# A hybrid decoder trunk on one core: the tables of its S5 groups built for two batches at once, their third one copied, one scaling moved to ScalarE

## The chip, the cores and the metric

The kernel runs on one core of a Trainium2 chip. The metric is the device time of one execution in microseconds (us), lower is better. A core has a tensor engine (PE), a vector engine (DVE), a scalar engine (ACT), GpSimd (POOL) and a sync engine (SP), which here issues nearly all DMAs. Each engine works through its own instructions in order and waits for others by semaphores.

## What is computed

A trunk of two layers over 1040 tokens (16 learned ones ahead of 1024) of width 1024, in float32. Layer 0 mixes the tokens by RG-LRU heads (512 channels) and by 32 S5 groups of 16 channels with 64 complex states each; layer 1 by a Mamba-2 mixer. A squared-ReLU MLP follows each mixer. What the change touches is the S5 part and one line of the RG-LRU:

```python
# S5, group g: a complex diagonal recurrence over the tokens
mag = exp(a_re * dt);  ar, ai = mag * cos(a_im * dt), mag * sin(a_im * dt)
fr = ((ar - 1) * a_re + ai * a_im) / den;  fi = (ai * a_re - (ar - 1) * a_im) / den
bbar = (fr + i fi) * b            # input vectors, 64 states x 16 channels
s[t] = (ar + i ai) * s[t - 1] + bbar @ u[t]
y[t] = Re(c @ s[t]) + d * u[t]
# RG-LRU
a = exp(log_a);  mult = sqrt(-expm1(2 * log_a));  h[t] = a[t] * h[t - 1] + mult[t] * (i[t] * x[t])
```

## The kernel before, in words

Tokens lie in three ranges of 400, 384 and 256 columns. Every dense product is made of three float32r products of 12-bit halves (`mm3`, lines 162 to 164) with features on the partitions; weights are loaded by SP into three buffers (`wraw`), split on ACT (line 156) and on DVE or POOL (line 157).

The first mixer (`mixer0`) runs 36 units of the input projection (12 output tiles by three token ranges). The first four tiles are the S5 channels (u0 to u3), then come those of the RG-LRU (x0 to x3) and its gates (g0 to g3). Between the units the program emits the work of the 32 S5 groups in eight batches of four: `s5_tables` makes the matrices of a batch, `s5_batch` its states and outputs, `s5_tile` the gelu and gate of 128 channels (two batches), and `lru_tile` the recurrence of 128 LRU channels. When all is there, the mixers' output is split and the output projection (`ev_out`) follows.

An S5 batch takes eight tokens at a time (130 chunks). Its state is turned by a phasor so that a real scan does the recurrence: `Z` holds cos and sin of 131 rotations for the four groups, built by doubling (2, 4, 8, 16, 32, 64, then 3 more columns; lines 557 to 559; steps below 32 on DVE, the wider ones on POOL). The partitions are 64 real and 64 imaginary rows, and both halves hold the same rotations. Lines 574 to 582 scale the batch's input and output vectors (64 elements per partition, nine DVE instructions). Three tables of 512 elements follow (lines 590 to 592, three instructions each): E (input), F and G (output; G on DVE for the first two batches, on POOL for the six others). PE turns E into M2 (lines 603, 604) and the taps into M1 (line 618). In `s5_batch`, PE makes two products (lines 643, 644), DVE multiplies them with `Z` (lines 647 to 649), scans (651), POOL and DVE multiply by sin and cos again (653, 654), and PE sums M1, F and G products (661 to 663). The chunks travel through DRAM (`ud`, `yd`).

The order on each engine is set by a list scheduler at build time, from the emission order with a few shifts; SP's queue is in order too, so a DMA that waits holds up those behind it.

Of the kernel before, what the change touches and what calls it, by code (L numbers as in the profile page):

```python
# [78 lines left out]
class Trunk:  # L79
    def __init__(self, ctx, tc, A, out, dbg=None):  # L80
# [189 lines left out]
    def apply(self, wname, i, off, w, rb):  # L270
        """hi, lo <- split of rmsnorm(h) * w"""
# [10 lines left out]
    def split(self, wname, i, k, off, w):  # L282
        """hi, lo <- split of h[:, k] * w; the norm's factor per token is left to the products"""
# [20 lines left out]
    def final(self, i):  # L304
        """the last norm, to the output"""
# [19 lines left out]
    def follow(self, nxt, tls, i):  # L325
        """queues the norm that comes after the residual stream of token range i is complete"""
# [13 lines left out]
    def up_unit(self, tls, ws, i, f, pool, tag, rbs):  # L340
        """one tile of the hidden layer for one token range, in two parts"""
# [21 lines left out]
    def mlp(self, layer, tls, mp, ahead, nxt, ep=None, early=None, rbs=None):  # L363
        """ahead: weights of the first two tiles; nxt: weight of the norm that follows;
        ep, early, rbs: a pool for the first range's hidden tiles, those that are there, norm factors"""
# [23 lines left out]
        def do_down(parts, i, last=False):  # L389
            """parts: (weights, hidden) of one or two blocks"""  # L390
# [3 lines left out]
            for n in range(KT):  # L394
# [35 lines left out]
    def s5_params(self, pool, keep):  # L430
        """what does not depend on the data (in two steps)"""
# [37 lines left out]
        # powers of lambda: index d holds lambda^(8-d)  # L469
# [7 lines left out]
        def cmul(dst, a, b, n):  # L477
            """powers dst.. = powers a.. * power b"""
# [12 lines left out]
        # input factors  # L491
# [17 lines left out]
        # sign: -1 on the real rows, +1 on the imaginary rows  # L509
# [4 lines left out]
        # unit phasors over 8 * 2^n chunks, n = 0..7: rows cos, -sin, sin; modulus over 8 steps  # L514
# [20 lines left out]
    def s5_tables(self, pool, b):  # L535
        """matrices and rotations of the groups NG*b .. NG*b+NG-1 (in three steps)"""
        nc, s5 = self.nc, self.s5
        v, e = nc.vector, nc.gpsimd
        gs = slice(NG * b, NG * b + NG)
        S4 = [P, NG, 8, 16]  # L540
        S3 = [P, NG, 16]
        # rotations exp(i theta8 m), m = 0..130: rows cos, sin
        Z = pool.tile([P, 2, NG, 131], F32, name="s5Z", bufs=2)
# [24 lines left out]
        xa, xb, ya, yb = (bc[:, i] for i in range(4))
        bw = lambda q: q[:, gs].unsqueeze(2).broadcast_to(S3)
        sg, ng = s5["sg"][:, 0:1], s5["sg"][:, 1:2]  # L570
        x1 = pool.tile(S3, F32, name="s5x1")
        x2 = pool.tile(S3, F32, name="s5x2")
        x3 = pool.tile(S3, F32, name="s5x3")
# [920 lines left out]
```

## Time and profile before

| what | us |
|---|---|
| median of 3 runs (lowest, highest) | 2868.11 (2867.05, 2870.88) |
| span of the profiled execution, first to last instruction | 2866.7 |
| own time of the profiled execution | not listed apart from the three runs; from 0.4 to 4.2 above its span by these |
| PE busy | 2751.3 (96%) |
| DVE busy | 1884.3 (66%) |
| ACT busy | 917.6 (32%) |
| POOL busy | 720.4 (25%) |

The page cuts the span into 40 slices of 71.7 us and gives the busy share of each in tenths. `PEclk` is the clock granted to the tensor engine in tenths of full speed. Spans of matmuls overlap in PE's pipeline, and those of short DVE instructions overlap a little too, so sums of single spans are above the busy time of a stretch.

### The profile page before, as it was taken

Reading aid. Unit: us, or ns where it says so; the run is one execution under the profiler, and the core shown is the slowest. Engines: PE = TensorE matmul, PEld = TensorE weight load, DVE = VectorE, ACT = ScalarE, POOL = GpSimd, SP = SyncE. Lnnn points to the kernel's source line nnn. Section 1 sums busy time; section 2 is a strip of 40 time slices with the busy share of each in tenths; the row PEclk is TensorE's granted clock in tenths of the full one; section 3 lists DMA queues with packets and bytes.
Section 4 is the critical chain, followed back from the end, with each engine's and each line's share of the span. In section 5 each row is a group of like instructions: output and inputs, shape, how many; then the busy total and the mean of one; then the engine's idle time right before and its main releaser. Section 6 shows DMA issues by size and latency. Waiting matters only on the chain.

```text
span 2866.7 us, 45283 instructions
## 1 busy us (share of the span) xinstructions
PE 2751.3 (96%) x17625; PEld 2684.1 (94%) x17625; DVE 1884.3 (66%) x4127; ACT 917.6 (32%) x1926; POOL 720.4 (25%) x879
## 2 busy tenths in 40 slices
PE   7877999999999999999999999999989999999998
PEld 7866999999999999899999999998889999999998
DVE  9999655555555555977867768677894555555554
ACT  4354542111211112454434434335452111121113
POOL 4555111101101011242333323334441011110112
PEclk9888999999999999999999999999999999999999
DMA  4111311110101111031212212213311111011111
GB/s 145 60 43 44 117 48 52 49 60 30 60 30 60 48 42 43 20 102 48 77 51 68 72 58 73 63 47 105 109 50 61 41 49 59 30 60 35 55 48 59
DMA packets 118919, 170.00 MB, mean 59 GB/s; under 512 B 17072, under 2 KB 51632, under 8 KB 118704
## 3 DMA queue, kind: packets, MB, share of 16 engines
q1 hardware_dynamic: 118416, 166.95, 18.1%
q8 instruction: 138, 2.26, 0.3%
q14 instruction: 77, 0.63, 0.1%
q10 hardware_dynamic: 288, 0.15, 0.0%
HBM read 158.34 MB, written 8.72 MB: 58 GB/s over the span
## 4 chain that ended last, share of the span: by engine, by line
PE 76%; DVE 17%; ACT 2%; issue 2%; DMA 2%; POOL 1%; SPq 0%; DVEq 0%; ACTq 0%; POOLq 0%
PE mm L163 23%; PE mm L162 23%; PE mm L164 23%; DVE xbc L1071 2%; DMA csb<-csd 1%; PE mm L1181 1%; PE sm L1185 1%; PE mm L1178 1%; DVE lo L288 1%; PE sm L1144 1%; PE sm L250 1%; PE sm L233 1%; DVE s5tt L591 1%; DVE wlo L157 0%; DVE h L697 0%
## 5 line engine op out<-in xcount | busy, mean ns | idle before, releaser
L162 PE MATMUL mm<-hi,whi 128*128 128x256 f32 (+2 forms) x2400 | 788.6, 329 | 9.2 <-ACT whi L156 8.5
L164 PE MATMUL mm<-hi,wlo 128*128 128x256 f32 (+2 forms) x2400 | 772.9, 322 | 3.2 <-POOL wlo L157 3.2
L163 PE MATMUL mm<-lo,whi 128*128 128x256 f32 (+2 forms) x2400 | 774.3, 323 | 1.2 <-POOL lo L280 0.6
L400 DVE TENSOR_TENSOR h<-h,mm 128x384 f32<-128x384 f32 (+1 forms) x720 | 369.0, 513 | 301.5 <-PE mm L164 299.5
L162 PEld LDWEIGHTS mm<-hi,whi 128*128 128x128 f32 x2400 | 457.5, 191 | 14.6 <-ACT whi L156 8.9
L164 PEld LDWEIGHTS mm<-hi,wlo 128*128 128x128 f32 x2400 | 456.8, 190 | 4.2 <-POOL wlo L157 3.9
L357 POOL TENSOR_TENSOR s<-s 128x384 f32<-128x384 f32 (+2 forms) x192 | 161.8, 843 | 1188.7 <-DVE s L356 946.3
L163 PEld LDWEIGHTS mm<-lo,whi 128*128 128x128 f32 x2400 | 456.1, 190 | 3.9 <-POOL lo L280 0.9
L163 PE MATMUL mm<-hl,dhi 128*128 128x384 f32 (+2 forms) x1440 | 459.5, 319 | 0.0
L164 PE MATMUL mm<-hh,dlo 128*128 128x384 f32 (+2 forms) x1440 | 459.4, 319 | 0.0
L162 PE MATMUL mm<-hh,dhi 128*128 128x384 f32 (+2 forms) x1440 | 459.3, 319 | 0.1
L156 ACT CAST dhi<-wraw 128x512 fp32r<-128x512 f32 x120 | 68.9, 620 | 653.7 <-PE mm L163 574.8
L162 PEld LDWEIGHTS mm<-hh,dhi 128*128 128x128 f32 x1440 | 271.9, 189 | 0.3 <-DVE h L400 0.3
L164 PEld LDWEIGHTS mm<-hh,dlo 128*128 128x128 f32 x1440 | 272.0, 189 | 0.0
L163 PEld LDWEIGHTS mm<-hl,dhi 128*128 128x128 f32 x1440 | 271.9, 189 | 0.0
L163 PE MATMUL mm<-lo,uhi 128*128 128x384 f32 (+2 forms) x768 | 245.3, 319 | 0.0
L164 PE MATMUL mm<-hi,ulo 128*128 128x384 f32 (+2 forms) x768 | 245.0, 319 | 0.0
L162 PE MATMUL mm<-hi,uhi 128*128 128x384 f32 (+2 forms) x768 | 244.9, 319 | 0.0
L1071 DVE SCALAR_TENSOR_TENSOR xbc<-s,cols,xbc 128x400 f32<-128x400 f32 (+2 forms) x288 | 202.5, 703 | 24.4 <-ACT xbc L1069 22.2
L358 ACT CAST hh<-s 128x384 fp32r<-128x384 f32 (+2 forms) x192 | 92.3, 480 | 384.4 <-POOL s L357 384.0
L359 DVE TENSOR_TENSOR hl<-s,hh 128x384 fp32r<-128x384 f32 (+2 forms) x192 | 99.5, 518 | 145.5 <-ACT hh L358 143.5
L356 DVE SCALAR_TENSOR_TENSOR s<-mm,rb 128x384 f32<-128x384 f32 (+2 forms) x192 | 98.9, 515 | 142.7 <-PE mm L164 139.5
(374 smaller groups left out, 4566.6 us busy)
## 6 DMA issues: line engine op xcount, KB each, us to landing
wraw<-in_mlp_up SPq DMA_DIRECT2D x128, 256.0 KB
wraw<-in_mlp_down SPq DMA_DIRECT2D x128, 256.0 KB
wraw<-in_ssd_in SPq DMA_DIRECT2D x120, 256.0 KB
csb<-csd SPq DMA_DIRECT2D x64, 256.0 KB
sa<-ecd SPq DMA_DIRECT2D x128, 64.0 KB
wraw<-in_ssd_out SPq DMA_DIRECT2D x32, 256.0 KB
wraw<-in_ev_in SPq DMA_DIRECT2D x24, 256.0 KB
wraw<-in_ev_out SPq DMA_DIRECT2D x18, 256.0 KB
```

Source lines behind the costliest of these rows:

```text
L156: nc.scalar.copy(hi[:, s], raw)
L162: nc.tensor.matmul(pt, lhsT=whi, rhs=xhi, start=first, stop=False)
L163: nc.tensor.matmul(pt, lhsT=whi, rhs=xlo, start=False, stop=False)
L164: nc.tensor.matmul(pt, lhsT=wlo, rhs=xhi, start=False, stop=last)
L233: nc.tensor.matmul(st[:l, 508 + i:509 + i], lhsT=a[:, o:o + l], rhs=self.ones, start=j == 0, stop=j == len(accs) - 1)
L250: self.nc.tensor.matmul(st[:, o:o + l], lhsT=y[:l, i:i + 1].broadcast_to([l, P]), rhs=self.ident[:l, :l], start=True, stop=True)
L356: nc.vector.scalar_tensor_tensor(out=r, in0=pt[:, :w], scalar=0.0, in1=rbs[i], op0=ALU.max, op1=ALU.mult)
L357: nc.gpsimd.tensor_tensor(out=sq, in0=r, in1=r, op=ALU.mult)
L358: nc.scalar.copy(hh, sq)
L359: nc.vector.tensor_tensor(out=hl, in0=sq, in1=hh.bitcast(F32), op=ALU.subtract)
L400: nc.vector.tensor_tensor(out=hs, in0=hs, in1=pt[:, :w], op=ALU.add)
L1071: v.scalar_tensor_tensor(out=ot, in0=raw[:, k:k + w], scalar=cw(k), in1=ot, op0=ALU.mult, op1=ALU.add)
```

## The change

- The vectors (old lines 574 to 582) are scaled once for all 32 groups, by `s5_vectors`: three ACT and six DVE instructions of 512 elements. One DMA of 1 MB brings them, in place of eight.
- The rotations of two batches are built at once (`s5_rotations`, called for even batches): the first batch on partitions 0 to 63, the second on 64 to 127, all steps on DVE. ACT makes a third row, minus sin, and four DMAs per pair copy the halves into the two batches' `Z`; the sign that line 648 applied is in that row now, so that line becomes a plain product.
- G is F with its partition halves exchanged: two DMAs per batch copy it.
- In `lru_tile` the scaling by 0.5 plus 0.5 (line 720) moves from DVE to ACT.
- The descriptor scratch of the program is set to 1024 bytes; comments are dropped, which moves line numbers.

```diff
+    def s5_vectors(self, pool):
...
+        nc.scalar.activation(out=xb, in_=xb, func=AF.Copy, scale=sg)
+        nc.scalar.activation(out=ya, in_=ya, func=AF.Copy, scale=ng)
+        nc.scalar.activation(out=yb, in_=yb, func=AF.Copy, scale=-1.0)
+        v.tensor_tensor(out=ta, in0=xa, in1=bw(s5["fi"]), op=ALU.mult)
+        v.tensor_tensor(out=tb, in0=xb, in1=bw(s5["fi"]), op=ALU.mult)
+        v.tensor_tensor(out=xa, in0=xa, in1=bw(s5["fr"]), op=ALU.mult)
+        v.tensor_tensor(out=xa, in0=xa, in1=tb, op=ALU.add)
+        v.tensor_tensor(out=xb, in0=xb, in1=bw(s5["fr"]), op=ALU.mult)
+        v.tensor_tensor(out=xb, in0=xb, in1=ta, op=ALU.subtract)
+
+    def s5_rotations(self, pool, b):
...
+        ph = pool.tile([P, 8, 3, NG], F32, name="s5phh")
+        for r in range(2):
+            g = NG * (b + r)
+            nc.scalar.copy(ph[r * H:(r + 1) * H], s5["ph"][r * H:(r + 1) * H, :, :, g:g + NG])
+        Z = pool.tile([P, 3, NG, 131], F32, name="s5Zh")
...
         while m < 131:
             l = min(m, 131 - m)
             S = [P, 2, NG, l]
...
-            e = v if m < 32 else nc.gpsimd
-            e.tensor_tensor(out=t1[:, :, :, :l], in0=Z[:, ::-1, :, 0:l], in1=pn, op=ALU.mult)
-            e.tensor_tensor(out=dst, in0=src, in1=pc, op=ALU.mult)
-            e.tensor_tensor(out=dst, in0=dst, in1=t1[:, :, :, :l], op=ALU.add)
+            v.tensor_tensor(out=t1[:, :, :, :l], in0=Z[:, 1::-1, :, 0:l], in1=pn, op=ALU.mult)
+            v.tensor_tensor(out=dst, in0=Z[:, 0:2, :, 0:l], in1=pc, op=ALU.mult)
+            v.tensor_tensor(out=dst, in0=dst, in1=t1[:, :, :, :l], op=ALU.add)
...
+        nc.scalar.activation(out=Z[:, 2], in_=Z[:, 1], func=AF.Copy, scale=-1.0)
+        for r in range(2):
+            q = self.rot[b + r] = pool.tile([P, 2, NG, 131], F32, name="s5Z", bufs=2)
+            nc.sync.dma_start(q[:H], Z[r * H:(r + 1) * H, 0:2])
+            nc.sync.dma_start(q[H:], Z[r * H:(r + 1) * H, 0:3:2])
...
-        v.tensor_scalar(out=xb, in0=xb, scalar1=sg, scalar2=None, op0=ALU.mult)
-        v.tensor_tensor(out=x1, in0=xa, in1=bw(s5["fr"]), op=ALU.mult)
-        v.tensor_tensor(out=x3, in0=xb, in1=bw(s5["fi"]), op=ALU.mult)
-        v.tensor_tensor(out=x1, in0=x1, in1=x3, op=ALU.add)
-        v.tensor_tensor(out=x2, in0=xb, in1=bw(s5["fr"]), op=ALU.mult)
-        v.tensor_tensor(out=x3, in0=xa, in1=bw(s5["fi"]), op=ALU.mult)
-        v.tensor_tensor(out=x2, in0=x2, in1=x3, op=ALU.subtract)
-        v.tensor_scalar(out=ya, in0=ya, scalar1=ng, scalar2=None, op0=ALU.mult)
-        v.tensor_scalar(out=yb, in0=yb, scalar1=-1.0, scalar2=None, op0=ALU.mult)
...
-        G = table("s5G", dn, yb, ya, ALU.subtract, v if b < 2 else e, "s5tt", 2)
+        G = pool.tile(S4, F32, name="s5G", bufs=2)
+        nc.sync.dma_start(G[:64], F[64:])
+        nc.sync.dma_start(G[64:], F[:64])
...
-            v.scalar_tensor_tensor(out=w2[sl], in0=v3(vb), scalar=ng, in1=Sn[sl], op0=ALU.mult, op1=ALU.mult)
+            v.tensor_tensor(out=w2[sl], in0=v3(vb), in1=Sn[sl], op=ALU.mult)
...
-            v.tensor_scalar(out=q[i], in0=q[i], scalar1=0.5, scalar2=0.5, op0=ALU.mult, op1=ALU.add)
+            nc.scalar.activation(out=q[i], in_=q[i], func=AF.Copy, scale=0.5, bias=0.5)
```

The scheduler makes a new order for the first mixer; behind it the engines' orders are as before. On DVE, at the tables of the third batch, there stood the last narrow doubling step and the vectors (`s5Z` is the batch's rotations, `s5bc` its vectors, `s5x` their products):

```order
L557 TENSOR_TENSOR s5t_1179<-s5Z,s5ph 128x8x16
L558 TENSOR_TENSOR s5Z<-s5Z,s5ph 128x8x16
L559 TENSOR_TENSOR s5Z<-s5Z,s5t_1179 128x8x16
L574 TENSOR_SCALAR s5bc<-s5bc,s5sg 128x64
L575 TENSOR_TENSOR s5x_1208<-s5bc,s5t_437 128x64
```

Now the wide steps of the second pair stand there, among the tables (`s5Zh` is the pair's rotations, `s5F`, `s5E` and `s5tt` the tables):

```order
L581 TENSOR_TENSOR s5t_1147<-s5Zh,s5phh 128x512
L582 TENSOR_TENSOR s5Zh<-s5Zh,s5phh 128x8x64
L610 TENSOR_TENSOR s5F<-s5t_409,s5bc 128x512
L583 TENSOR_TENSOR s5Zh<-s5Zh,s5t_1147 128x8x64
L612 TENSOR_TENSOR s5F<-s5F,s5tt 128x512
L581 TENSOR_TENSOR s5t_1147<-s5Zh,s5phh 128x8x3
```

The vectors have moved ahead, to one place before the first batch, and the wide steps have come over from POOL.

In SP's queue, between the second batch's chunks and the outputs of the first, there stood:

```order
L155 DMA wraw<-in_ev_in 128x512 x2
L768 DMA ud_112<-ux 128x1040
L666 DMA yd_113<-s5yg 8x16x130 x4
L565 DMA s5bc<-in_s5bc 128x4x64
L567 DMA s5dm<-in_s5dm 128x64
L632 DMA s5ug<-ud_110 128x1x130 x4
L155 DMA wraw<-in_ev_in 128x512 x3
```

Now the next weights stand among copies of G and `Z`, of which the second pair of `Z` copies (lines 589 and 590 after G) needs the buffer of the batch before:

```order
L654 DMA s5ug<-ud_110 128x1x130 x4
L634 DMA s5G<-s5F 64x512
L589 DMA s5Z<-s5Zh 64x1048
L590 DMA s5Z<-s5Zh 64x2x524
L635 DMA s5G<-s5F 64x512
L155 DMA wraw<-in_ev_in 128x512 x2
L589 DMA s5Z<-s5Zh 64x1048
L590 DMA s5Z<-s5Zh 64x2x524
L155 DMA wraw<-in_ev_in 128x512
```

Weight loads and chunk transfers that had DMAs from DRAM ahead of them now have copies ahead that wait for DVE and ACT.

## Rows read from the trace of the kernel before

**Rows 1.** The page, part 2: busy tenths in 40 slices of 71.7 us.

```profile
PE   7877999999999999999999999999989999999998
...
DVE  9999655555555555977867768677894555555554
...
PEclk9888999999999999999999999999999999999999
```

**Rows 2.** Windows: stretch, length, busy us (instructions) of PE, PEld, DVE, ACT, POOL, clock, DMA.

```profile
45.00:285.00 240.00, 189.65 (x1101) 174.90 (x1101) 224.53 (x503) 99.75 (x185) 130.34 (x141) 0.86 0.19 57
285.00:316.00 31.00, 29.82 (x176) 28.09 (x174) 24.41 (x47) 17.97 (x35) 5.29 (x5) 0.87 0.11 32
316.00:440.00 124.00, 120.30 (x759) 118.57 (x759) 71.20 (x145) 53.15 (x111) 21.38 (x20) 1.00 0.31 101
```

**Rows 3.** What PE waited for, 45 to 316 us: total us, times, longest.

```profile
PE mm L644 <- DVE ux L774: 10.1, 3, 6.3
PE sm L618 <- DVE s5kk L610: 7.7, 5, 2.2
...
PE sm L233 <- DVE sa L267: 0.2, 1, 0.2
```

**Rows 4.** Lines by form, DVE, 0 to 440 us: busy us, mean ns | idle before.

```profile
L580 DVE TENSOR_TENSOR s5x<-s5x,s5x 128x64 f32<-128x64 f32 x8 | 5.5, 684 | 0.0
...
L575 DVE TENSOR_TENSOR s5x<-s5bc,s5t 128x64 f32<-128x64 f32 x8 | 1.8, 224 | 0.0
```

**Rows 5.** Timeline, DVE at 160.5 us: start, span.

```profile
160.56 0.22 DVE L558 TENSOR_TENSOR s5Z<-s5Z,s5ph 128x64 f32<-128x64 f32 x1
160.69 0.22 DVE L577 TENSOR_TENSOR s5x<-s5x,s5x 128x64 f32<-128x64 f32 x1
```

**Rows 6.** Lines by form, DVE, 0 to 440 us: the narrow doubling steps.

```profile
L557 DVE TENSOR_TENSOR s5t<-s5Z,s5ph 128x16 f32<-128x16 f32 x8 | 4.4, 555 | 0.0
...
L558 DVE TENSOR_TENSOR s5Z<-s5Z,s5ph 128x16 f32<-128x16 f32 x8 | 1.4, 171 | 0.0
```

**Rows 7.** The same, the tables, the scaling and the line behind it.

```profile
L590 DVE TENSOR_TENSOR s5F<-s5t,s5bc 128x512 f32<-128x512 f32 x8 | 10.8, 1349 | 0.0
...
L592 DVE TENSOR_TENSOR s5F<-s5F,s5tt 128x512 f32<-128x512 f32 x8 | 6.2, 774 | 0.1
...
L721 DVE SCALAR_TENSOR_TENSOR l_tr<-h 128x400 f32<-128x400 f32 x4 | 4.9, 1224 | 0.1
...
L720 DVE TENSOR_SCALAR h<-h 128x400 f32<-128x400 f32 x4 | 3.1, 768 | 0.0
...
L721 DVE SCALAR_TENSOR_TENSOR l_tr<-h 128x384 f32<-128x384 f32 x4 | 2.2, 548 | 0.0
...
L720 DVE TENSOR_SCALAR h<-h 128x256 f32<-128x256 f32 x4 | 1.1, 285 | 0.0
```

**Rows 8.** Line 592's own instructions: duration min/median/max in ns, first and last start.

```profile
L592 DVE TENSOR_TENSOR s5F<-s5F,s5tt x8: 671/686/1411, 68.2 to 279.8; 128x512 f32<-128x512 f32 x8
L592 DVE TENSOR_TENSOR s5G<-s5G,s5tt x2: 681/686/692, 69.7 to 92.2; 128x512 f32<-128x512 f32 x2
```

**Rows 9.** Lines by form, POOL, 0 to 440 us: wide doubling steps, table G.

```profile
L559 POOL TENSOR_TENSOR s5Z<-s5Z,s5t 128x512 f32<-128x512 f32 x8 | 11.7, 1457 | 0.4
...
L590 POOL TENSOR_TENSOR s5G<-s5t,s5bc 128x512 f32<-128x512 f32 x6 | 8.7, 1450 | 0.6 <-issue 0.4
...
L591 POOL TENSOR_TENSOR s5tt<-s5t,s5bc 128x512 f32<-128x512 f32 x6 | 7.8, 1306 | 10.5 <-DVE s5F L592 10.5
...
L558 POOL TENSOR_TENSOR s5Z<-s5Z,s5ph 128x24 f32<-128x24 f32 x8 | 2.9, 362 | 19.1 <-DVE s5Z L559 7.7 <-DMA s5dm<-in_s5dm 4.7 <-DVE s5y L219 4.1
```

**Rows 10.** SP's queue: one issue with its time; its longest wait.

```profile
69.74 0.60 SPq L565 DMA_DIRECT2D s5bc<-in_s5bc  x1
SPq L155 <- DVE wlo L157: 122.4, 23, 26.2
```

**Rows 11.** The chain of waits: a transfer of 520 KB on the path.

```profile
316.06 3.38 DMA s5y<-yd
```

**Rows 12.** All waits, 0 to 440 us: how long one batch holds up its successor.

```profile
POOL s5w L653 <- DVE s5w L651: 39.3, 7, 12.6
```

More of the change, by code (lines that the diff above doesn't have):

```diff
@@ L508, in s5_params @@
         tt(fi, den, ALU.mult, fi, e)
+        bc = keep.tile([P, 4, 32, 16], F32, name="s5bc")
+        nc.sync.dma_start(bc, self.A["s5bc"].rearrange("p a (g i) -> p a g i", i=16))
         sg = keep.tile([P, 2], F32, name="s5sg")
@@ L525, in s5_params @@
         v.tensor_scalar(out=ph[:, :, 1], in0=ph[:, :, 2], scalar1=-1.0, scalar2=None, op0=ALU.mult)
-        self.s5 = dict(pr=pr, pi=pi, fr=fr, fi=fi, rho=rho, phs=[ph[:, n] for n in range(8)], sg=sg)
+        self.s5 = dict(pr=pr, pi=pi, fr=fr, fi=fi, rho=rho, ph=ph, sg=sg, bc=bc)
     def csquare(self, o, q, x):
@@ L533, in csquare @@
         v.tensor_tensor(out=o[:, 0], in0=x[:, 0], in1=x[:, 1], op=ALU.subtract)
-    def s5_tables(self, pool, b):
+    def s5_vectors(self, pool):
         nc, s5 = self.nc, self.s5
[L538 to L543, printed above, removed]
+        v = nc.vector
+        S = [P, 32, 16]
+        bc = s5["bc"]
+        xa, xb, ya, yb = (bc[:, i] for i in range(4))
+        bw = lambda q: q.unsqueeze(2).broadcast_to(S)
+        sg, ng = s5["sg"][:, 0:1], s5["sg"][:, 1:2]
+        ta = pool.tile([P, NG, 8, 16], F32, name="s5E").rearrange("p g j i -> p (g j i)").rearrange("p (g i) -> p g i", i=16)
+        tb = pool.tile([P, NG, 8, 16], F32, name="s5tt").rearrange("p g j i -> p (g j i)").rearrange("p (g i) -> p g i", i=16)
+        nc.scalar.activation(out=xb, in_=xb, func=AF.Copy, scale=sg)
[8 more added lines that the diff above has]
+    def s5_rotations(self, pool, b):
+        nc, s5 = self.nc, self.s5
+        v = nc.vector
+        H = P // 2
+        ph = pool.tile([P, 8, 3, NG], F32, name="s5phh")
[3 more added lines that the diff above has]
+        Z = pool.tile([P, 3, NG, 131], F32, name="s5Zh")
         t1 = pool.tile([P, 2, NG, 64], F32, name="s5t1")
-        e.memset(Z[:, 0, :, 0:1], 1.0)
-        e.memset(Z[:, 1, :, 0:1], 0.0)
-        e.tensor_copy(Z[:, :, :, 1], s5["phs"][0][:, 0:3:2, gs])
+        v.memset(Z[:, 0, :, 0:1], 1.0)
+        v.memset(Z[:, 1, :, 0:1], 0.0)
+        v.tensor_copy(Z[:, 0:2, :, 1], ph[:, 0, 0:3:2])
         m, n = 2, 1
@@ L560, in s5_tables @@
+            pn = ph[:, n, 1:3].unsqueeze(3).broadcast_to(S)
+            dst = Z[:, 0:2, :, m:m + l]
+            v.tensor_tensor(out=t1[:, :, :, :l], in0=Z[:, 1::-1, :, 0:l], in1=pn, op=ALU.mult)
+            v.tensor_tensor(out=dst, in0=Z[:, 0:2, :, 0:l], in1=pc, op=ALU.mult)
+            v.tensor_tensor(out=dst, in0=dst, in1=t1[:, :, :, :l], op=ALU.add)
             m += l
             n += 1
-        e = nc.gpsimd
-        bc = pool.tile([P, 4, NG, 16], F32, name="s5bc")
-        nc.sync.dma_start(bc, self.A["s5bc"].rearrange("p a (g i) -> p a g i", i=16)[:, :, gs])
+        nc.scalar.activation(out=Z[:, 2], in_=Z[:, 1], func=AF.Copy, scale=-1.0)
@@ L566, in s5_tables @@
+        for r in range(2):
+            q = self.rot[b + r] = pool.tile([P, 2, NG, 131], F32, name="s5Z", bufs=2)
+            nc.sync.dma_start(q[:H], Z[r * H:(r + 1) * H, 0:2])
+            nc.sync.dma_start(q[H:], Z[r * H:(r + 1) * H, 0:3:2])
+    def s5_tables(self, pool, b):
+        nc, s5 = self.nc, self.s5
+        v = nc.vector
+        gs = slice(NG * b, NG * b + NG)
+        S4 = [P, NG, 8, 16]
+        if b % 2 == 0:
+            self.s5_rotations(pool, b)
         dm = pool.tile([P, NG * 16], F32, name="s5dm")
@@ L567, in s5_tables @@
         nc.sync.dma_start(dm, self.A["s5dm"][:, b])
[L568 to L573, printed above, removed]
-        v.tensor_scalar(out=xb, in0=xb, scalar1=sg, scalar2=None, op0=ALU.mult)
-        v.tensor_tensor(out=x1, in0=xa, in1=bw(s5["fr"]), op=ALU.mult)
@@ L576, in s5_tables @@
-        v.tensor_tensor(out=x3, in0=xb, in1=bw(s5["fi"]), op=ALU.mult)
-        v.tensor_tensor(out=x1, in0=x1, in1=x3, op=ALU.add)
-        v.tensor_tensor(out=x2, in0=xb, in1=bw(s5["fr"]), op=ALU.mult)
-        v.tensor_tensor(out=x3, in0=xa, in1=bw(s5["fi"]), op=ALU.mult)
-        v.tensor_tensor(out=x2, in0=x2, in1=x3, op=ALU.subtract)
-        v.tensor_scalar(out=ya, in0=ya, scalar1=ng, scalar2=None, op0=ALU.mult)
-        v.tensor_scalar(out=yb, in0=yb, scalar1=-1.0, scalar2=None, op0=ALU.mult)
+        x1, x2, ya, yb = (s5["bc"][:, i, gs] for i in range(4))
@@ L585, in s5_tables, with table @@
         up, dn = slice(1, 9), slice(0, 8)
-        def table(name, sl, c1, c2, op, eng, tt, bufs):
+        def table(name, sl, c1, c2, bufs):
             o = pool.tile(S4, F32, name=name, bufs=bufs)
-            t = pool.tile(S4, F32, name=tt)
-            eng.tensor_tensor(out=o, in0=pw(s5["pr"], sl), in1=cw(c1), op=ALU.mult)
-            eng.tensor_tensor(out=t, in0=pw(s5["pi"], sl), in1=cw(c2), op=ALU.mult)
-            eng.tensor_tensor(out=o, in0=o, in1=t, op=op)
+            t = pool.tile(S4, F32, name="s5tt")
+            v.tensor_tensor(out=o, in0=pw(s5["pr"], sl), in1=cw(c1), op=ALU.mult)
+            v.tensor_tensor(out=t, in0=pw(s5["pi"], sl), in1=cw(c2), op=ALU.mult)
+            v.tensor_tensor(out=o, in0=o, in1=t, op=ALU.add)
             return o
-        E = table("s5E", up, x1, x2, ALU.add, v, "s5tt", 1)
+        E = table("s5E", up, x1, x2, 1)
         yield
@@ L610, in s5_tables @@
         v.tensor_tensor(out=ks, in0=kk[:, :NG * 16], in1=dm, op=ALU.add)
-        F = table("s5F", dn, ya, yb, ALU.add, v, "s5tt", 2)
-        G = table("s5G", dn, yb, ya, ALU.subtract, v if b < 2 else e, "s5tt", 2)
-        self.tab[b] = [M2, F, G, Z]
+        F = table("s5F", dn, ya, yb, 2)
+        G = pool.tile(S4, F32, name="s5G", bufs=2)
+        nc.sync.dma_start(G[:64], F[64:])
+        nc.sync.dma_start(G[64:], F[:64])
+        self.tab[b] = [M2, F, G, self.rot.pop(b)]
         yield
```

11 lines of the change are left out of this document (4 added, 7 removed).

## The prediction

> **What bounds the kernel now.** I read the slices first [rows 1]. PE is at 9 tenths or more nearly everywhere, with one weak stretch that lasts: the first four slices, at 7 to 8, where DVE stands at 9 and the granted clock at 8 or 9. That is the first mixer, and the change touches nothing else: behind it the order of every engine is as before. So only this stretch can give time, and whatever it gives is kept, because PE is at 97% from 316 us on [rows 2] and simply starts that work earlier.
>
> Then the windows [rows 2]. From 45 to 285 us, 240 us, DVE is busy for 224.5 us (93.5%) and PE for 189.7 (79%), at a clock of 0.86. From 285 to 316 PE is busy for 29.8 of 31: there PE already bounds. The stretch before 45 us is the start, with stages that the change leaves nearly alone. So 240 us are at stake, and DVE sets their length. The waits say the same [rows 3]: between 45 and 316 us the 13 rows of PE's waits sum to 51.3 us, and the ten of them that name DVE to 45.9. None names weights: these come in time today.
>
> Last, why DVE is slow. The same 512-element product takes 0.67 to 0.69 us in its best cases and 1.4 in others [rows 8]; line 590 for F averages 1.35 [rows 7]. POOL is busy for 130 of the 240 us [rows 2], mostly with two-input products. What a DVE instruction costs here depends on what POOL does beside it.
>
> **The change, part by part, on DVE.**
> - Vectors: nine rows of 8 instructions, from L580's 5.5 us to L575's 1.8, sum to 31.7 us [rows 4]. Short instructions start 0.13 us apart with spans of 0.22 [rows 5], so 0.08 of each span is shared: 72 times 0.08 is 5.8, and 26 us go. Six instructions of 512 elements come, each 0.68 less the same 0.08: 3.6 us, once, before the first batch. Their 1 MB DMA is issued among the first loads, tens of us before it is read; three ACT instructions are hidden, ACT being busy for 100 of 240 us [rows 2].
> - Rotations: twelve rows of narrow steps, from 4.4 to 1.4 us, sum to 27.6, or 21 without the shared part [rows 6]. Half as many remain: about 8 us, taking the middle of their prices without POOL beside them (0.06 to 0.25 us apart). The wide steps come over from POOL, four times nine instructions. The nearest DVE row for the 512-element ones is 0.60 (0.68 less 0.08) [rows 8], half of it for 256 elements, 0.1 for 24: 4 x 3 x (0.60 + 0.33 + 0.10) = 12.4. Net about -1 us. If they cost what tables cost beside POOL (1.35), it is +8; that end is kept.
> - G on DVE for two batches: six instructions of about 0.65, -4 us [rows 8].
> - The scaling (line 720): twelve instructions, 3.1 us for 400 columns down to 1.1 for 256, with 2.5 between: 6.7, less the shared part 6 us. On ACT they are about 0.5 us each, behind the exponential that ACT itself makes, so they add no new engine to that chain.
> - POOL's share in the others: POOL loses nine rows of doubling steps, 60.7 us from 11.7 to 2.9, and three rows of G, 24.9, from 8.7 to 7.8 [rows 9]: some 86 of its 130 us. The tables' six DVE rows, 48 instructions of E and F, took about 51 us (the first and the last of the six: [rows 7]); at 0.60 each they are 29. Two thirds of these 22 us, by POOL's share that goes: -15. Other lines suffer as well (line 721: 1224 ns for 400 columns, 548 for 384 [rows 7]): I take -6, from 2.5 us for that line alone, and from zero to twice that as its ends.
>
> Sum on DVE: -26 + 3.6 - 1 - 4 - 6 - 15 - 6 = **-54 us**, leaving about 170 of 224.5. Without any relief from POOL, and with the dear wide steps, it is -24 and leaves 200.
>
> **On the queue and the path.** SP gets 33 DMAs (16 of `Z`, 16 of G, one of 1 MB) and loses 8: 25 more at 0.60 us to issue [rows 10], 15 us of 240, which is room that SP has: it sat waiting for free weight buffers for 122 us. A copy of 131 to 262 KB lands somewhat sooner than the 520 KB that took 3.4 us [rows 11]; with ACT's negation ahead of it, `Z` arrives some 4 us after its last step. In the new order, 10 DVE instructions of tables (6 us) stand between the first pair's last step and its first use, and over thirty for the later pairs. So I cost the copies at nothing; the cover is those instructions, and if it were gone, 4 us per pair, 16 in all, would come back. G is used a batch's states later than F, further than that. Each pair's `Zh` buffer is rewritten only after its copies left; the wait is on DVE, and the table and convolution rows behind it would wait too.
>
> What if the copies of a pair do not overlap each other? By the 3.4 us for 520 KB, one of 262 KB takes about 1.7, and four in turn 6.8: 5 us more per pair, 20 us in all, if nothing covers them. That mechanism goes into rival 2. The Trainium skill, "DMA: Bandwidth & Descriptors", section "Rules for kernel authors", says so outright: two transfers to disjoint partition halves serialize, and one over all partitions is better. No run here shows such a pair yet; by that rule, without cover, the sum would be 17 us and not 37.
>
> **From DVE to time.** With 170 us on DVE, PE's 189.7 us is the larger. The engine that bounds reached 93.5% today, by the windows; I let PE reach the same at the same clock: 189.7 / 0.935 = 203 us in place of 240, **-37 us**. This hardly hangs on the relief: with 200 us left on DVE, 200 / 0.935 = 214, -26. The profiled execution had a span of 2866.7 us; the median of the runs is 1.4 above it, and I keep that: 2866.7 - 37 + 1.4 = **2831 us**.
>
> **The rivals.**
> 1. *The clock comes back.* It was 0.86 where PE kept waiting and 1.00 from 316 us on, where PE was at 97% [rows 2]. If closer work raises it to 1.00, PE needs 189.7 x 0.86 = 163 us, and DVE's 170 bounds: 170 / 0.935 = 182, -58: **2810 us**. Against it: even 285 to 316 us, at 96% PE, had only 0.87.
> 2. *Two engines near their limit take turns.* PE and DVE both do about 180 us and each waits for the other in order; at 85% of the larger, 189.7 / 0.85 = 223, -17: **2851 us**. The new hop through ACT and SP adds to it, as would copies in turn (20 us back leaves the same 17).
> 3. *SP's queue becomes the wait: slower.* The second `Z` copies wait until the batch before has let its buffer go, and weights and chunks stand behind them. A batch kept its successor waiting for 12.6 us at most [rows 12]. If each of the four pairs holds weights back by that much plus a landing of 3.4, PE loses 64 us against 37 gained: +27, **2895 us**. It decides once a pair costs over 9 us. For it: the order shows the weights behind. Against: today no PE wait names weights, and SP waited 122 us only because the buffers ahead were still full.
> 4. *Nothing moves:* the copies return what DVE gains, **2868 us**. DVE's own share in PE's waits, 46 us, speaks against it.
>
> **How the numbers follow.** A measurement of this kernel tells about 0.2%, 5.7 us, from no change. The forecast, -25 to -50 us, has 0.50; rival 1, beyond -50, 0.15; rival 2, -6 to -25, 0.22; rival 3 0.08; rival 4 0.05. So faster 0.87, same 0.05, slower 0.08. The range of 2807 to 2855 takes in the forecast, nearly all of rival 1 and two thirds of rival 2: about 0.8. The bounds of the DVE sum (-26 us of time at the dear end) lie inside it.
>
> **What would show it.** Right: rotations and G gone from POOL, which falls by some 86 us; lines that were 590 to 592 near 0.7 us each; DVE's busy time in the first 290 us down by 45 to 60; the S5 and input stage ending near 248 us in place of 285, the same PE work behind it; PE's waits on DVE down from 46 to about 15 us. Wrong: PE waits that name weights or `s5Z`, DVE waits on `s5Zh` copies of more than 4 us each, or tables still at 1.3 us with POOL quiet.

## The result and the profile after

| | median of 4 runs, us (lowest to highest) |
|---|---|
| before | 2868.84 (2867.05 to 2870.88) |
| changed | 2833.41 (2831.17 to 2836.82) |
| ratio | 0.9878, 95% interval 0.9865 to 0.989 |

The change takes 35.4 us off, 1.2%. The profiled execution took 2833.13 us, its span is 2831.4. The page of the changed kernel, parts 1 and 2 (busy us by engine, then busy tenths in 40 slices):

```profile
PE 2740.4 (97%) x17625; PEld 2676.8 (95%) x17625; DVE 1832.7 (65%) x4043; ACT 927.5 (33%) x1953; POOL 626.5 (22%) x765
...
PE   7998999999999999999999999999899999999998
...
DVE  9887465555555556776876767778884555555555
...
POOL 2212121101010113243332333324441111010112
PEclk9989999999999999999999999999999999999999
```

Against [rows 1] slices 2 to 4 of PE are one or two tenths higher, and behind them PE differs nowhere by more than a tenth. Over the whole span DVE loses 51.6 us (1884.3 to 1832.7), POOL 93.9 (720.4 to 626.5) and PE 10.9 (2751.3 to 2740.4, for the same 17625 matmuls). So of the 35 us, 11 are PE's own busy time, with a higher granted clock in this stretch, and some 24 are time in which PE no longer stands still.

Windows of the changed kernel, columns as in [rows 2]:

```profile
45.00:250.00 205.00, 184.19 (x1149) 171.37 (x1150) 171.97 (x420) 109.34 (x212) 41.71 (x34) 0.93 0.35 93
250.00:285.00 35.00, 29.22 (x171) 27.75 (x170) 28.12 (x51) 21.13 (x42) 5.78 (x4) 0.90 0.17 47
285.00:405.00 120.00, 116.65 (x734) 115.29 (x733) 69.14 (x149) 48.51 (x101) 20.79 (x20) 1.00 0.31 101
```

The stretch of 240 us [rows 2] is answered by one of 205 (at its end the whole kernel is 35 us ahead; it holds 1149 matmuls where the old one held 1101, since the order is new): PE is busy for 90% of it (79% before), DVE for 84% (93.5% before), and the clock is 0.93 instead of 0.86. The engine that is fullest has changed, as forecast.

What PE waited for from 45 to 285 us, the longest and the last of fifteen rows:

```profile
PE mm L162 <- DVE s5w L669: 5.7, 1, 5.7
PE mm L703 <- ACT s L701: 5.3, 1, 5.3
PE sm L641 <- DVE s5kk L630: 3.4, 3, 1.6
PE mm L683 <- DVE ux L796: 2.8, 4, 0.9
...
PE sm L233 <- DVE sa L267: 0.2, 1, 0.2
```

The sum is 26 us, 21 of it on DVE (before: 51.3 and 45.9); none names weights or `s5Z`. The line groups on DVE, 0 to 405 us (busy us, mean ns of one | idle before), that answer to [rows 6 to 8]:

```profile
L611 DVE TENSOR_TENSOR s5tt<-s5t,s5bc 128x512 f32<-128x512 f32 x16 | 11.8, 737 | 0.1
...
L582 DVE TENSOR_TENSOR s5Zh<-s5Zh,s5phh 128x16 f32<-128x16 f32 (+6 forms) x28 | 11.3, 408 | 0.0
...
L610 DVE TENSOR_TENSOR s5E<-s5t,s5bc 128x512 f32<-128x512 f32 x8 | 6.2, 778 | 0.0
L612 DVE TENSOR_TENSOR s5F<-s5F,s5tt 128x512 f32<-128x512 f32 x8 | 6.1, 759 | 0.0
...
L610 DVE TENSOR_TENSOR s5F<-s5t,s5bc 128x512 f32<-128x512 f32 x8 | 5.5, 682 | 0.0
```

Line 590 for F, 1349 ns in [rows 7], is line 610 for F here, 682 ns.

### The profile page after: what moved, and what is told of

The parts are those of the page before. It is cut to its first block, busy times and chain, and to the rows that moved or that the text cites. A ratio compares the mean times of both kernels' runs of the same rounds, so it can differ in the third digit from the quotient of the medians.

```text
span 2831.4 us, 45178 instructions
## 1 busy us (share of the span) xinstructions
PE 2740.4 (97%) x17625; PEld 2676.8 (95%) x17625; DVE 1832.7 (65%) x4043; ACT 927.5 (33%) x1953; POOL 626.5 (22%) x765
## 4 chain that ended last, share of the span: by engine, by line
PE 77%; DVE 15%; ACT 2%; issue 2%; DMA 2%; POOL 1%; SPq 0%; DVEq 0%; POOLq 0%; ACTq 0%
PE mm L163 24%; PE mm L162 24%; PE mm L164 23%; DVE xbc L1094 3%; DMA csb<-csd 1%; PE mm L1204 1%; DVE lo L288 1%; PE sm L1208 1%; PE mm L1201 1%; PE sm L1167 1%; PE sm L250 1%; DVE wlo L157 1%; DVE zs L1230 1%; PE sm L233 0%; DVE xbc L1096 0%
## 5 line engine op out<-in xcount | busy, mean ns | idle before, releaser
L1094 DVE SCALAR_TENSOR_TENSOR xbc<-s,cols,xbc 128x400 f32<-128x400 f32 (+2 forms) x288 | 205.4, 713 | 25.6 <-ACT xbc L1092 23.5
```

The source lines that it names most:

```text
L1094: v.scalar_tensor_tensor(out=ot, in0=raw[:, k:k + w], scalar=cw(k), in1=ot, op0=ALU.mult, op1=ALU.add)
```

## The experiments

Each run's median, its ratio to runs of the kernel before on the same chip, and the busy time of DVE and POOL over the whole span. The list scheduler orders every engine anew for each edit, so a run differs from its neighbour in more than the edited lines. In the last 2540 us, where the work is the same, DVE's busy time still differs between runs by a few us (1582 to 1591) and POOL's by ten (555 to 565); smaller differences say nothing.

| run | kernel | median us | ratio (95% interval) | DVE | POOL |
|---|---|---|---|---|---|
| | before | 2868.84 | 1 | 1884.3 | 720.4 |
| | changed | 2833.41 | 0.9878 (0.9865 to 0.989) | 1832.7 | 626.5 |
| 1 | before + vectors for all groups | 2866.40 | 0.9995 (0.9986 to 1.0004) | 1845.0 | 705.0 |
| 2 | before + rotations on DVE, two batches | 2845.39 | 0.992 (0.9907 to 0.9934) | 1853.4 | 657.3 |
| 3 | before + G by copies | 2847.41 | 0.9924 (0.991 to 0.9939) | 1858.1 | 687.7 |
| 4 | before + LRU scaling on ACT | 2865.55 | 0.9986 (0.9977 to 0.9995) | 1876.0 | 720.4 |
| 5 | changed + loose products on POOL | 2883.27 | 1.005 (1.0036 to 1.0063) | 1863.1 | 705.7 |
| 6 | changed + products on DVE | 2835.80 | 0.9886 (0.9872 to 0.9899) | 1843.7 | 637.5 |
| 7 | changed, vectors per batch | 2829.16 | 0.9863 (0.985 to 0.9877) | 1842.8 | 626.5 |
| 8 | run 1 + own temporaries for POOL | 2859.36 | 0.9967 (0.9955 to 0.998) | 1862.3 | 713.5 |
| 9 | changed + products on POOL, tied to their batch | 2861.94 | 0.9979 (0.997 to 0.9988) | 1860.2 | 701.2 |
| 10 | changed + memsets on POOL, tied the same way | 2837.60 | 0.9894 (0.9878 to 0.991) | 1833.1 | 700.8 |
| 11 | before + rotations and G alone | 2831.16 | 0.9869 (0.9853 to 0.9886) | 1842.4 | 627.9 |
| 12 | run 11 + the scan's product on DVE | 2827.31 | 0.9852 (0.9835 to 0.9869) | 1840.2 | 618.4 |

### Runs 1 to 4: one part of the change at a time

Run 1 adds `s5_vectors` and its early DMA to the kernel before (and the smaller descriptor scratch, as run 2 does):

```diff
-        bc = pool.tile([P, 4, NG, 16], F32, name="s5bc")
...
+        x1, x2, ya, yb = (s5["bc"][:, i, gs] for i in range(4))
...
+            self.s5_vectors(m0)
```

> The kernel before, with the vectors for all groups at once and nothing else of the change. Theory (VectorE sets the length of the first mixer, so what it loses there comes off the time): its nine rows of short instructions go (26 us) and six long ones come (3.6 us), so -22 on VectorE and, at the 0.935 that the bound engine reached, about -24 us: 2845. Rival (TensorE and VectorE take turns, so a saving on one engine only counts in part): half of that, about -11: 2858. Rival (nothing is kept, the stage is paced otherwise): within 0.2%.

Measured: no difference, though DVE lost 39.3 us. What DVE waited for in run 1, from 45 to 330 us:

```profile
DVE l_ti L723 <- ACT l_ti L719: 10.1, 3, 5.1
DVE s5tt L597 <- POOL s5G L598: 8.4, 2, 6.5
DVE s5w L660 <- POOL s5w L659: 7.2, 6, 1.2
DVE s5t L580 <- POOL ux L779: 6.2, 1, 6.2
DVE s5t L580 <- POOL s5Z L582: 6.0, 1, 6.0
```

Before, DVE's only wait of that size was the third (7.2 us, for the scan's product on POOL). Now it also waits 20.6 us for POOL's G and rotations, and 10.1 us for ACT in the RG-LRU (the first row). The timeline of run 1 around the first of the 6 us waits (start, span):

```profile
87.44 0.68 DVE L596 TENSOR_TENSOR s5E<-s5t,s5bc 128x512 f32<-128x512 f32 x1
...
93.76 0.23 POOL L580 TENSOR_TENSOR s5t<-s5Z,s5ph 128x24 f32<-128x24 f32 x1
94.07 0.24 POOL L582 TENSOR_TENSOR s5Z<-s5Z,s5t 128x24 f32<-128x24 f32 x1
94.25 0.10 POOL L779 MEMSET ux<- 128x3 f32 x1
...
94.35 0.18 DVE L580 TENSOR_TENSOR s5t<-s5Z,s5ph 128x16 f32<-128x16 f32 x1 [6.22 <-POOL ux L779]
```

DVE's next narrow step writes `s5t`, of which there is one tile, and POOL reads it until 94.3 us. The profile names the memset, POOL's last instruction before; that it is really the tile is what run 8 tests.

Run 2 builds the rotations on DVE for two batches and copies them:

```diff
+            v.tensor_tensor(out=t1[:, :, :, :l], in0=Z[:, 1::-1, :, 0:l], in1=pn, op=ALU.mult)
...
-            e = v if m < 32 else nc.gpsimd
```

Run 3 copies G and leaves out the sign of one half of it:

```diff
-        G = table("s5G", dn, yb, ya, ALU.subtract, v if b < 2 else e, "s5tt", 2)
+        G = pool.tile(S4, F32, name="s5G", bufs=2)
+        nc.sync.dma_start(G[:64], F[64:])
+        nc.sync.dma_start(G[64:], F[:64])
```

> The kernel before, with the rotations of two batches at once on VectorE and the copies, and nothing else (both halves of the rotation get the rows cos and sin by plain copies; the negated row is not made on ScalarE but the before-form of its use is kept). GpSimd loses its 60.7 us of wide steps. Theory (contention: what GpSimd does beside VectorE makes VectorE's two-input instructions longer): VectorE's direct change is about -1 us, but the tables on lines 590 to 592 fall from 1.3 us to under 1.0 and -12 to -15 us of VectorE time come from that, so about -14 us: 2855. Rival (the price of a table hangs on something else): tables stay at 1.3 us, time 2865 to 2876. Rival (copies in turn are on the path): +5 to +20 on top, TensorE or VectorE waits that name s5Z.

> The kernel before, with G copied from F by two DMAs per batch and no other change; the sign of one half of G is left as it is in F, so G's values differ from the reference there, while all other work is the same. VectorE loses six instructions (4 us), GpSimd 24.9 us of its three-fold products from the third batch on. Theory: -4 directly, a quarter of the relief (some -5), so -8 to -10 us: 2860. Rival without contention: -4: 2865. Rival copies on the path: TensorE waits on s5G, up to +20.

Measured: -23 us and -22 us by the ratios, each far above what was expected of it (-14, -10). Page, part 1, of run 2:

```profile
PE 2745.7 (97%) x17625; PEld 2680.0 (94%) x17625; DVE 1853.4 (65%) x4127; ACT 923.8 (32%) x1938; POOL 657.3 (23%) x783
```

and of run 3:

```profile
PE 2742.7 (96%) x17625; PEld 2680.3 (94%) x17625; DVE 1858.1 (65%) x4121; ACT 921.5 (32%) x1929; POOL 687.7 (24%) x861
```

By count DVE's own work barely changes: run 2 has as many instructions on it as before (4127), run 3 six fewer. Yet DVE's busy time falls by 30.9 and 26.2 us. No wait of PE or DVE names the copies.

Run 4:

```diff
-            v.tensor_scalar(out=q[i], in0=q[i], scalar1=0.5, scalar2=0.5, op0=ALU.mult, op1=ALU.add)
+            nc.scalar.activation(out=q[i], in_=q[i], func=AF.Copy, scale=0.5, bias=0.5)
```

> The kernel before, with the LRU scaling on ScalarE and nothing else: twelve VectorE instructions go (6 us). Theory of a VectorE bound: -6 us, 2863. Rival (the LRU stands where TensorE already bounds, or in the chain of one unit): within 0.1%, 2866 to 2869.

Measured: -4 us, interval -1.4 to -6.6; between the two.

What follows: the parts that took work off POOL carry the gain; the one that took most off DVE alone carries none.

### Runs 6, 7 and 11: does DVE still set the length, and do the vectors count once POOL is quiet?

Run 6 adds products to DVE in the changed kernel:

```diff
+        for _ in range(4):
+            v.tensor_tensor(out=d1, in0=d1, in1=s5["pr"][:, 0, 0:1].broadcast_to([P, 512]), op=ALU.mult)
```

> The changed kernel with four more 512-element products per batch on VectorE, 32 in all, on data that nothing else uses: at 0.60 us each 19 us of VectorE's time. Theory (after the change TensorE bounds the first mixer, VectorE has some 15% of room): a third of it or less comes through, 0 to 7 us: 2833 to 2840. Rival (VectorE still sets the length): 19 / 0.935 = 20 us: 2853.

Measured: 2.4 us, not to be told from nothing. The dummies are there (line groups of run 6 by form, 0 to 330 us):

```profile
L618 DVE TENSOR_TENSOR s5d<-s5d,s5t 128x512 f32<-128x512 f32 x32 | 21.9, 685 | 3.1 <-issue 3.1
```

Their net weight is smaller than their spans: DVE's busy time rises by 11.0 us and not by 19, and POOL's in the first 330 us from 73.2 to 81.0, for the same 76 instructions. But 11.0 us at 0.935 would still be 12 us of time, and the two intervals leave no more than 8. So DVE has room for them, and PE sets the length.

Run 7 puts the per-batch vectors back into the changed kernel, as they were before:

```diff
+        v.tensor_scalar(out=xb, in0=xb, scalar1=sg, scalar2=None, op0=ALU.mult)
+        v.tensor_tensor(out=x1, in0=xa, in1=bw(s5["fr"]), op=ALU.mult)
...
+        v.tensor_scalar(out=yb, in0=yb, scalar1=-1.0, scalar2=None, op0=ALU.mult)
...
-            self.s5_vectors(m0)
```

Run 11 puts the LRU scaling back on DVE as well:

```diff
-            nc.scalar.activation(out=q[i], in_=q[i], func=AF.Copy, scale=0.5, bias=0.5)
+            v.tensor_scalar(out=q[i], in0=q[i], scalar1=0.5, scalar2=0.5, op0=ALU.mult, op1=ALU.add)
```

> The changed kernel with the vectors computed per batch again, as before (72 short instructions instead of six long ones and one early DMA); all else as in the change. The vectors alone gave nothing on the kernel before. Theory A (there VectorE ran into waits for GpSimd, whose work is gone here, so the same saving counts now): slower than the change by 8 to 20 us: 2841 to 2853. Theory B (with GpSimd relieved, TensorE bounds, and VectorE's 22 us lie in its room): within 5 us of the change: 2828 to 2838. Theory C (single parts add up, -23 and -22 and -4): faster than the change, 2820 to 2826.

> Of the change only the rotations (on VectorE, two batches at once) and G by copies; vectors per batch and the LRU scaling on VectorE as before. Theory (all that counts is what leaves GpSimd; vectors and LRU scaling lie in VectorE's room): as fast as the whole change, 2827 to 2836. Rival (the LRU scaling counts, -4 alone): 2835 to 2840. Rival (vectors and scaling count together once GpSimd is quiet): above 2840.

Measured: 0.9863 and 0.9869 against 0.9878, three overlapping intervals. Theory B and the first theory hold: rotations and G are the whole gain, and vectors and scaling lie in DVE's room. The singles do not add up (-23 and -22, together -38), as is to be expected when PE bounds by then. Line groups by form of run 7, DVE, 0 to 330 us, the dearest and the cheapest of the nine vector rows:

```profile
L588 DVE TENSOR_SCALAR s5bc<-s5bc,s5sg 128x64 f32<-128x64 f32 x8 | 2.7, 339 | 0.0
...
L594 DVE TENSOR_TENSOR s5x<-s5x,s5x 128x64 f32<-128x64 f32 x8 | 1.7, 217 | 0.0
...
L596 DVE TENSOR_SCALAR s5bc<-s5bc 128x64 f32<-128x64 f32 x8 | 1.5, 188 | 0.0
```

Line 594 here is line 580 of [rows 4], the same eight instructions: 684 ns there, 217 here. The nine rows sum to 16.9 us instead of 31.7. Nearly half of what the vectors cost before was POOL's doing.

### Run 8: the hand-overs over shared temporaries

Run 8 gives POOL's steps and POOL's G temporary tiles of their own, in the kernel of run 1:

```diff
-            e = v if m < 32 else nc.gpsimd
+            e, t1 = (v, tv) if m < 32 else (nc.gpsimd, tp)
...
-        G = table("s5G", dn, yb, ya, ALU.subtract, v if b < 2 else e, "s5tt", 2)
+        G = table("s5G", dn, yb, ya, ALU.subtract, v if b < 2 else e, "s5tt" if b < 2 else "s5tg", 2)
```

> The kernel before with the vectors for all groups at once, and with temporary tiles of its own for GpSimd's rotation steps and for GpSimd's third table (two more tiles of 2 KB per partition), nothing else. With the vectors alone VectorE idled 20.6 us for GpSimd in three waits (8.4, 6.2 and 6.0 us) that end at the shared temporaries. Theory of hand-overs: these waits go, and 10 to 20 us of time with them: 2848 to 2858. Rival, contention: with the waits gone GpSimd works beside VectorE more often, its instructions get longer, and the time stays within 4 us of the vectors alone: 2862 to 2870.

Measured: 2859.4, 7 us below run 1 and between the two forecasts: neither holds alone. The three waits of 20.6 us are gone from the list, so they did hang on the two tiles; but DVE's busy time rises from 1845.0 to 1862.3 us for the same 4061 instructions. Most of what the waits gave back is spent again by working beside POOL.

### Runs 5, 9 and 10: what POOL's work costs

Run 5 puts products on scratch data back on POOL, as many and as long as the wide steps and G were:

```diff
+        for l in (32, 64, 3):
+            for _ in range(3):
+                nc.gpsimd.tensor_tensor(out=d1[:, :, :, :l], in0=d1[:, :, :, :l], in1=s5["ph"][:, 0:2, 0:1, 0:NG].rearrange("p a c g -> p a g c").broadcast_to([P, 2, NG, l]), op=ALU.mult)
...
```

> The changed kernel with GpSimd's removed work put back as products on data that nothing else uses: nine per batch with the sizes of the wide rotation steps, three of 512 per batch from the third on; the outputs are the same. The products hold the engine and work beside VectorE as before, but VectorE hands nothing to them and waits for none of them; only what stands behind them on GpSimd's queue can be late. Theory of contention (GpSimd's work makes VectorE's instructions longer, and this is what its removal gave): the tables go back from 0.7 to about 1.1 us, VectorE's busy time in the first 290 us rises by 35 to 45 us, and the time by 15 to 25 us: 2848 to 2858. Rival, hand-overs (before, VectorE and GpSimd waited for each other over shared temporary tiles and in-order steps, and this is what the removal gave): VectorE's spans get longer as well, but the time rises by 8 us at most: 2833 to 2841.

Measured: +50 us on the changed kernel, outside every expectation and slower than before. Since the products waited for nothing, the scheduler put those of several batches in front: POOL was busy for 101.1 of the first 150 us (37.9 in the changed kernel), ahead of the weights' splits and the scan's product. What DVE waited for longest in run 5, 0 to 330 us:

```profile
DVE s5w L684 <- POOL s5w L683: 25.7, 8, 17.3
```

and PE:

```profile
PE mm L692 <- DVE s5w L684: 15.1, 1, 15.1
PE mm L162 <- ACT whi L156: 7.9, 1, 7.9
```

As a test of contention the run is spoiled: it adds to it the price of standing in front on an in-order queue. So run 9 has the same products behind F, tied to it by one element:

```diff
+        nc.scalar.copy(d1[:, 0, 0, 0:1], F[:, 0, 0, 0:1])
+        for l in (32, 64, 3):
...
```

and run 10 memsets in their places:

```diff
+        nc.scalar.copy(d1[:, 0:1], F[:, 0, 0, 0:1])
+        for w, n in ((341, 6), (588, 6), (346, 3)):
+            for _ in range(n):
+                nc.gpsimd.memset(self.d1[:, :w], 0.0)
...
```

> The changed kernel with the same 90 dummy products on GpSimd as in the run before (nine per batch, three more from the third on), but each batch's can start only once its table F is there (ScalarE copies one element of F into the dummy tile first), so they no longer bunch at the start, ahead of the weights' splits; they stand near where GpSimd's own wide steps stood before the change. Outputs are the same. Theory (what GpSimd does beside VectorE, together with the room it takes in its own queue, is what the change removed): most of the 35 us comes back, 2855 to 2872. Rival (the removed work was mainly bad by the hand-overs over shared temporaries, which these products don't have): 2833 to 2845.

> As the run with the tied products, in the same places and for about the same time (a 512-element product of 1165 ns is two memsets of 588 elements, and so on; a memset of 512 took 524 ns), but memsets, which read nothing. GpSimd is as busy and its queue as long. If the price of VectorE's instructions beside GpSimd (the tables at 0.9 to 1.1 us instead of 0.68) is what counts: near the changed kernel, 2833 to 2842, and the tables stay near 0.7 us. If the room on GpSimd's queue counts (what stands behind: the scan's product, the weights' splits): as the tied products, within 4 us of them.

Measured: +28.5 us with products, +4.2 with memsets. Page, part 1, of run 9:

```profile
PE 2752.3 (96%) x17625; PEld 2688.9 (94%) x17625; DVE 1860.2 (65%) x4043; ACT 931.0 (33%) x1962; POOL 701.2 (25%) x856
```

and of run 10:

```profile
PE 2749.2 (97%) x17625; PEld 2685.2 (95%) x17625; DVE 1833.1 (65%) x4043; ACT 931.4 (33%) x1963; POOL 700.8 (25%) x922
```

POOL is equally busy, DVE has the same 4043 instructions, and its busy time is 27.1 us longer beside the products. Beside the memsets it is that of the changed kernel (1832.7). The difference isn't one line's: of the line groups, 0 to 330 us, run 9 has

```profile
L612 DVE TENSOR_TENSOR s5E<-s5E,s5tt 128x512 f32<-128x512 f32 x8 | 7.7, 957 | 0.0
L583 DVE TENSOR_TENSOR s5Zh<-s5Zh,s5t 128x512 f32<-128x512 f32 x4 | 4.0, 1000 | 0.0
...
L636 POOL TENSOR_TENSOR s5d<-s5d,s5ph 128x512 f32<-128x512 f32 x24 | 27.3, 1137 | 1.8
```

and run 10

```profile
L612 DVE TENSOR_TENSOR s5E<-s5E,s5tt 128x512 f32<-128x512 f32 x8 | 6.5, 812 | 0.0
L583 DVE TENSOR_TENSOR s5Zh<-s5Zh,s5t 128x512 f32<-128x512 f32 x4 | 2.7, 687 | 0.0
...
L636 POOL MEMSET s5d<- 128x588 f32 x48 | 28.3, 590 | 2.3
```

So the room on POOL's queue is worth some 4 us, and 24 of the 28 hang on what POOL's instructions do, not on how long they take. The orders of the two runs are not the same, so single instructions must bear this out, and they do. Timeline of the kernel before (start, span), a product of POOL and one of DVE, of the same size:

```profile
202.31 1.10 POOL L590 TENSOR_TENSOR s5G<-s5t,s5bc 128x512 f32<-128x512 f32 x1
202.35 1.60 DVE L590 TENSOR_TENSOR s5F<-s5t,s5bc 128x512 f32<-128x512 f32 x1
```

DVE's starts 0.04 us after POOL's and ends 0.55 us after it, as if it had waited for POOL's end and then done its own work. In the kernel before, 54 DVE products of this form start in the first 325 us. 23 of them take longer than 0.9 us, and each of the 23 started while a product of POOL ran and ended 0.54 to 0.56 us after it. Of the other 31, twelve started in the last 0.3 us of such a product, and only one, beside line 653, earlier. In run 9, 14 of 66 are that long, ten of them behind the added products. In run 10, 19 of 66 started while a memset ran, and none of the 19 is longer than 0.9 us; the three that are stood behind products. In the changed kernel four of 66 are left, all behind POOL's product of the RG-LRU (line 739).

The Trainium skill, "SBUF — State Buffer", section "Who interferes with whom", says that a DVE instruction with two SBUF inputs contends with a GpSimd instruction that reads SBUF, and not with one that only writes it; runs 9 and 10 agree, with 1860.2 against 1833.1 us of DVE's time.

### Run 12: a version that goes further the same way

Run 12 takes one more product off POOL:

```diff
-        nc.gpsimd.tensor_tensor(out=w2[:, :, 0:130], in0=w[:, :, 0:130], in1=Sn[:, :, 0:130], op=ALU.mult)
+        v.tensor_tensor(out=w2[:, :, 0:130], in0=w[:, :, 0:130], in1=Sn[:, :, 0:130], op=ALU.mult)
```

> Rotations and G only, and in addition the product behind the scan (w2 = w times sine, eight instructions of 1.6 us on GpSimd) on VectorE, where it should take some 0.7 us; VectorE waited 7 us for it in the changed kernel. Theory (each thing that leaves GpSimd counts, and VectorE has room): 3 to 8 us faster than the run with rotations and G alone: 2822 to 2828. Rival (TensorE bounds, nothing more to get): within 3 us of it.

Measured: 2827.3, the lowest of all and 1.5% below the kernel before. Against run 11 it is 4 us, with overlapping intervals, so neither forecast is excluded. The groups, by form, 0 to 330 us, on POOL in run 11 and on DVE here:

```profile
L669 POOL TENSOR_TENSOR s5w<-s5w,s5Z 128x520 f32<-128x520 f32 x8 | 12.8, 1603 | 83.5 <-issue 53.6 <-DVE s5w L667 17.1 <-PE mm L164 12.8
```

```profile
L669 DVE TENSOR_TENSOR s5w<-s5w,s5Z 128x520 f32<-128x520 f32 x8 | 5.6, 695 | 0.0
```

## Why the prediction was right, and where it was not

The forecast was 2831 us and the result 2833. The frame held; its largest term did not.

- **Where the time is.** Right: only the first mixer moved, 240 us to 205, and the end of the kernel comes 35 us earlier.
- **DVE's sum, -54 us.** Measured -51.6 over the span. Right as a sum, wrong in its parts; that the errors cancel is luck.
- **Vectors, -26 + 3.6.** The term that failed. It took the nine rows' spans for the price of the instructions themselves. Run 7 shows that with POOL quiet they are 16.9 us and not 31.7, and DVE's net gain by this part is 10.1 us (1842.8 less 1832.7) and not 22. And none of it was time: run 1 gave nothing on the kernel before, run 7 nothing on the changed one.
- **POOL's relief, -15 and -6.** Mis-sized. Runs 2 and 3 have -30.9 and -26.2 on DVE where the same steps forecast -1 and -4 beside the relief; together (run 11) DVE loses 41.9, so the relief is about 37 us, not 21. Two thirds of the tables' excess was a fair guess for the tables; "other lines suffer as well" was the part to look at: the vectors alone carried 15.
- **The wide steps and tables on DVE.** Right in the main: the tables' rows average 0.68 to 0.78 us and those of the wide steps of 512 elements 0.69 to 0.90, and the dear end of 1.35 did not come. All rotation steps together have spans of 30.2 us (8.6, 11.3 and 10.3 on the three lines), or 23.5 less the shared 0.08 each; the prediction had 8 and 12.4.
- **G, -4, and the scaling, -6.** G's share of time was -22, through POOL. The scaling gave 4 us alone and nothing that shows beside the rest.
- **Copies at nothing.** Right for the whole: no listed wait of PE or DVE names `s5Z` or `s5G`, and the time is not 17 but 35 us lower, so the cover held. For the first pair it only just held. `Z` of its first batch landed 5.5 us after the last rotation step, not 4 (71.1 to 76.6 us), and DVE read it at 76.7. The half copies do run one after the other: by their packets in the trace, the four of the first pair moved from 72.3 to 73.8, 74.4 to 76.1, 76.0 to 77.5 and 77.2 to 78.9 us, 6.6 us in all (the prediction's estimate was 6.8). Two of a later batch, issued within 0.5 us of each other, took 2.9 us together, where one alone took 1.5. This agrees with the rule of the Trainium skill, "DMA: Bandwidth & Descriptors", section "Rules for kernel authors", that the prediction set against its own zero; the cover is why it cost nothing.
- **PE takes over at 93.5%, same clock.** The first half is right (run 6). The size came out by two errors that cancel, which is luck: PE reached only 90%, but the clock rose from 0.86 to 0.93, so that 184.2 us of work were left (for 48 matmuls more) and not 189.7. 184.2 / 0.90 is 205; the prediction had 203. PE's waits on DVE fell to 21 us, not 15.
- **Rivals.** The first happened in part: the clock rose, and 11 of the 35 us are PE's own. The second shows in the 90%. The third's mechanism exists: up to 285 us SP stood at line 589 for 13.0 us until line 676, the last reader of a `Z`, was done, and 14.4 us more behind two other DVE instructions; but no wait of PE in this stretch names weights. The fourth is out.

The chain that the runs support: before, DVE's instructions stood still until POOL's two-input products were done, and DVE's slowness kept PE waiting. Taking them off POOL ended both, until PE itself set the pace. Put back in place, they bring 28.5 of the 35 us again (run 9).

What stays open. Run 1 frees 39 us of DVE and gains nothing. 20.6 us went into waits for POOL and 10.1 into a wait for ACT, and run 8 shows that lifting the former brings 7 us; why the rest gave no time was not settled, nor how much of it is the new order of the instructions. The smaller descriptor scratch was not tried alone, but run 1 has it and gained nothing, and run 3 gained 22 us without it. Run 9's tables came to 0.68 to 0.96 us and not back to 1.35, so its products do not stand beside exactly the same DVE work as the originals did.

## What to carry to other kernels

When DVE looks like the bound and POOL works beside it, price DVE's instructions by their best cases first: here most of what lay above them was waiting for a product of POOL, in short lines as in long ones, and it went when that work left POOL. Look at the longest and shortest of a group and not at its mean. Taking cheap instructions off DVE gave nothing here, while moving POOL's two-input products onto DVE can make both the busy time of DVE and the kernel shorter. Before summing parts, ask which engine bounds once the first of them is done: here two parts of four gave the whole gain.

## What the runs showed of the hardware that was not expected

- 76 us of products on POOL (the four rows of dummies in run 9 sum to 76.2) cost DVE 27 us, more than a third of their own time; about as long a stretch of memsets (77.3 us) cost it nothing that shows. It goes the other way too: beside run 6's products on DVE, POOL's 76 instructions of the first 330 us took 81.0 us instead of 73.2.
- What a DVE instruction loses is what is left of POOL's product, however short it is itself. The eight of line 580, kernel before (ns min/median/max), of which [rows 4] shows the mean:

```profile
L580 DVE TENSOR_TENSOR s5x<-s5x,s5x x8: 210/644/1215, 59.7 to 271.9; 128x64 f32<-128x64 f32 x8
```

Four of the eight took 210 to 228 ns, as in run 7 (217 on average). The other four took 1059 to 1215, and each of these ended 0.08 us after the POOL product under which it had started. It isn't so every time: one of the four short ones also started while POOL's line 653 ran.

- The mean granted clock, between the levels of 1.2 and 2.4 GHz, was 0.86 before and 0.88 in run 9 (45 to 285 us), and 0.93 in the changed kernel (45 to 250 us), where PE had waited least; in the stretches that follow from 316 us on before and from 285 us on after it is 1.00.
